# Values of four heads in one projection: 512 weight columns moving, half of the tokens at a time

## The chip, the cores and the metric

The kernel runs on one core of a Trainium2 chip. The metric is device time in microseconds of one launch; lower is better. Matrix products run on TensorE (PE in the profile), their results lie in eight PSUM banks of 128 x 512 floats; VectorE (DVE), ScalarE (ACT) and GpSimd (POOL) do elementwise work; SyncE (SP) issues nearly all DMAs, in one queue and in order.

## The reference

One decoder layer, all in float32, for 1024 tokens of width 2048, with 8 stick-breaking heads and 8 retention heads of 128 columns each:

```python
mod = silu(c) @ w_ada + b_ada                       # shift, scale, gate
h   = rms_norm(x, norm_gain) * (1 + scale) + shift  # 1024 x 2048
proj = h @ w_in                                     # 2048 x 8192
q_sb, k_sb, v_sb, z_sb, q_r, k_r, v_r, z_r = split(proj)   # 1024 columns each
oa = stick_breaking(rms_norm(q_sb), rms_norm(k_sb), v_sb) * silu(z_sb)
ob = group_norm(retention(rotary(q_r), rotary(k_r), v_r)) * silu(z_r)
out = x + gate * (concat(oa, ob) @ w_out)
```

## The kernel before

Every large product is made from two float32r parts of each operand, a high part and the exact rest, in three matmuls (`mm3`, L132): high by high, high by low, low by high. The normed and conditioned input is kept as `h_hi` and `h_lo`, transposed (2048 features on partitions, in 16 blocks `kc`), in SBUF for the whole projection. Weights are streamed: `wchunk` (L124) takes a raw tile of 128 x 512 floats (tag `wr`, three buffers), loads 256 KB into it from SP's queue, and `split_w` (L116) makes the high part on ACT (L119) and the low part on DVE (L121), each in one of three buffers (tags `wh` and `wl`). Weight chunks are given a high priority (`AHEAD`), so that the scheduler of ACT, DVE and SP places them early. TensorE's order is the order of the program.

Two kinds of unit use this stream. `unit_t` (L139) makes one head's 128 columns of queries, keys or z, transposed: weights stationary, 512 tokens moving, two PSUM banks (tag `pj`, four banks), four chunks of four feature blocks. `unit_v` (L156) makes values, tokens by columns: 128 tokens stationary, 256 weight columns (two heads) moving, two blocks of tokens to a bank, so that the eight blocks of tokens fill the four `pj` banks; eight chunks of two feature blocks. There are eight such units, `v0`, `v2`, `v4`, `v6` and `rv0`, `rv2`, `rv4`, `rv6`.

The units are TensorE's steady work. After every second block each of them yields, and `tick` (L181) then lets the waiting tasks take a step: the norms of queries and keys, the heads' attention, and in the retention stage `z_bias` (L506) and `gate_parts` (L529). A task says after how many ticks it wants to go on. `z_bias` is started just before the first retention values; it loads 32 pieces of `w_in` into raw tiles of the tag `wr` (L516), two a step, a step every second tick, and sums them on DVE (L519, L521). `gate_parts` is started just behind the first retention values; it loads 64 pieces of `w_ada` into the same raw tiles (L490), one every third tick, eight to a part, and sums them on DVE (L494, L496).

What becomes of the values differs by stage. For the stick-breaking heads `spill_v` (L571) copies the four banks to staging tiles (tag `T`, four buffers, shared with the attention's `a_hi` and `a_lo`) and writes them to DRAM (`vraw`), from where `load_v` (L599) brings each head's values back. For the retention heads `evac_v` (L457) copies the banks straight into the two heads' tiles (tag `V`, two buffers). The retention attention (L797) first turns keys (`turn_k`), and after a gap of five ticks uses the values in `states` (L812), then `scores`, `values` and `finish`. Each retention head's queries and keys are rotated (L787) with cosines and sines that are loaded once, at the start of the retention stage (L784, L785).

At the end `out_unit` (L749) makes the output, 512 columns of `w_out` moving and tokens stationary, with a raw tile for each chunk of weights; its first two parts, `0a` and `0b`, take half of the tokens each and also load the concatenated heads back from DRAM through raw tiles (L742).

Of the kernel before, what the change touches and what calls it, by code (L numbers as in the profile page):

```python
# [55 lines left out]
def layer_kernel(ctx, tc, x, c, w_ada, b_ada, norm_gain, w_in, sb_q_gain, sb_k_gain, ret_norm_gain, w_out,  # L56
# [50 lines left out]
    def rsqrt_newton(y, m, u, iters=3):  # L107
        """y = m ** -0.5 from the exponent trick and Newton's iteration (u is room for a product)."""
        nc.vector.tensor_scalar(y.bitcast(I32), m.bitcast(I32), -0.5, RSQRT_MAGIC, op0=ALU.mult, op1=ALU.add)
        for _ in range(iters):  # L110
            nc.vector.tensor_tensor(u, y, y, op=ALU.mult)
            nc.vector.scalar_tensor_tensor(u, u, -0.5, m, op0=ALU.mult, op1=ALU.mult)
            nc.vector.scalar_tensor_tensor(y, u, 1.5, y, op0=ALU.add, op1=ALU.mult)

# [22 lines left out]
    h_hi, h_lo = {}, {}  # by block of 128 features and half of the tokens  # L137

    def unit_t(col0, halves, name, lo_pool=()):  # L139
        """(w_in[:, col0:col0+128]).T @ h.T, 512 tokens a bank. Yields between its steps; returns the banks."""  # L140
        o = {hf: ps.tile([P, HALF], F32, tag="pj", bufs=4, name=f"pj_{name}_{hf}") for hf in halves}
        for kq in range(4):
            def parts(raw):
                yield raw.rearrange("p (k n) -> p k n", n=P), w_in_k[:, 4 * kq:4 * kq + 4, col0:col0 + P]
            with tc.high_priority(AHEAD):
                hi, lo = wchunk(parts, f"{name}_{kq}", nc.gpsimd if kq in lo_pool else nc.vector)
            for hf in halves:
                for k in range(4):
                    kc = 4 * kq + k
                    sl = slice(k * P, (k + 1) * P)  # L150
                    mm3(o[hf], hi[:, sl], lo[:, sl], h_hi[kc, hf], h_lo[kc, hf], kc == 0, kc == KC - 1)
                    if k % 2:
                        yield
        return o

    def unit_v(col0, name):  # L156
        """h @ w_in[:, col0:col0+256]: two heads' values, two blocks of tokens a bank."""
        o = [ps.tile([P, HALF], F32, tag="pj", bufs=4, name=f"pv_{name}_{b}") for b in range(4)]
        for kk in range(8):
            def parts(raw):  # L160
                yield raw.rearrange("p (k n) -> p k n", n=2 * P), w_in_k[:, 2 * kk:2 * kk + 2, col0:col0 + 2 * P]
            with tc.high_priority(AHEAD):
                hi, lo = wchunk(parts, f"{name}_{kk}")
            for tb in range(NB):
                for k in range(2):
                    kc = 2 * kk + k
                    sl = slice(k * 2 * P, (k + 1) * 2 * P)
                    tk = slice(tb % 4 * P, (tb % 4 + 1) * P)
                    mm3(o[tb // 2][:, (tb % 2) * 256:(tb % 2) * 256 + 256],
                        h_hi[kc, tb // 4][:, tk], h_lo[kc, tb // 4][:, tk], hi[:, sl], lo[:, sl],  # L170
                        kc == 0 and tb % 2 == 0, kc == KC - 1 and tb % 2 == 1)
                if tb % 2:
                    yield
        return o

    # The projections are TensorE's steady work; the heads' tasks put their small products between
    # its steps, each some steps after the one whose results it needs.
# [31 lines left out]
    # The conditioning's scale is loaded before its shift. Until the shift is known h.T stands without it,  # L209
    # and what is projected from that (the first NZ retention heads' z) gets its share later (z_bias).  # L210
# [5 lines left out]
    vraw = [dr.tile([P, NB, 2, P], F32, name=f"vraw{i}") for i in range(NH // 2)]  # L216
    zb = cons.tile([P, 8], F32, name="zb")
    with tc.tile_pool(name="st", bufs=1) as st:
# [7 lines left out]
        def load_ada(cc, gs=range(4)):  # L226
            """A chunk of 256 columns of w_ada: eight chunks of the scale, then eight of the shift."""
            col = (D if cc < 8 else 0) + (cc % 8) * 2 * P
            for g in gs:
                ada[cc, g] = ar = st.tile([P, 4, 2 * P], F32, tag="ada", bufs=ADA_BUFS, name=f"ada_{cc}_{g}")  # L230
                nc.sync.dma_start(ar, ada_rows[:, 4 * g:4 * g + 4, col:col + 2 * P])
# [12 lines left out]
        def x_scale(ts, ss):  # L244
            """x over its rows' root mean squares, for some blocks of tokens."""
# [15 lines left out]
        def x_turn(kc, g, tag, bufs):  # L261
            """Half of a block of x.T, into the place that the next block of h.T's low part takes over."""
# [10 lines left out]
        def ada_sums(cc):  # L273
            """Sums of silu(c) w_ada over a partition's sixteen rows, for a chunk of 256 columns."""
# [20 lines left out]
        def ada_mod(cc, acc):  # L295
            """Sums over the partitions: (scale + 1) gain, or shift, for two blocks of h.T."""
# [10 lines left out]
        def make_h(kc, hf):  # L307
            """h.T without its shift."""
# [149 lines left out]

    def evac_v(o, idx):
        vt = []  # L460
        for e in range(2):
            v = com.tile([P, NB, P], F32, tag="V", bufs=2, name=f"v_{idx + e}")
            vt.append(v)
        with tc.high_priority(AHEAD):
            for b in range(4):
                src = o[b].rearrange("p (t e n) -> p t e n", t=2, e=2)
                for e in range(2):
                    dst = vt[e][:, 2 * b:2 * b + 2, :]
                    nc.scalar.activation(dst, src[:, :, e, :], AF.Copy)  # L469
        return vt  # L470
# [13 lines left out]
    def gate_part(h, pool):  # L484
        """The gate's columns 256 h to 256 (h + 1), without their bias, to gate_row."""
# [22 lines left out]
    def z_bias():  # L508
        """The shift's share in the first NZ retention heads' z, to zb."""
# [56 lines left out]
    def split_r(r, name):  # L566
        """A tile's two exact parts, by halves."""
        parts = [com.tile([P, S], F32R, tag="R", bufs=6, name=f"{n}_{name}") for n in ("rh", "rl")]
        return parts

    def spill_v(o, h, pool):  # L571
        """Two heads' values to DRAM, as they stand in the banks."""
        with tc.high_priority(AHEAD):
            for b in range(4):
                vt = pool.tile([P, HALF], F32, tag="T", bufs=4, name=f"vt_{h}_{b}")
                nc.scalar.activation(vt, o[b], AF.Copy)
                nc.sync.dma_start(vraw[h // 2][:, 2 * b:2 * b + 2].rearrange("p t e n -> p (t e n)"), vt)
# [3 lines left out]
    def sb_attention(h, q, k, pool, gap):  # L581
        # The heads' steps: a block of 128 queries over a chunk of 512 keys. Two blocks of queries
        # go together into the product with the values.
# [15 lines left out]
        def load_v():  # L599
            assert done_heads[0] == h  # L600
            for hf in range(2):
                bl = slice(hf * 4, hf * 4 + 4)
                raw = wp.tile([P, 4, P], F32, tag="wr", bufs=3, name=f"vr_{h}_{hf}")
                nc.sync.dma_start(raw, vraw[h // 2][:, bl, h % 2, :])
                nc.scalar.activation(v_hi[:, bl], raw, AF.Copy)
                nc.vector.tensor_tensor(v_lo[:, bl], raw, v_hi[:, bl].bitcast(F32), op=ALU.subtract)
# [32 lines left out]
        def turn(s):  # L639
            """Transposes into banks of two blocks of keys by two blocks of queries; after the second, splits."""  # L640
# [61 lines left out]
    vs = {}  # L702
    with tc.tile_pool(name="sb", bufs=1) as sb:
        for h in range(NH):
# [15 lines left out]
            if h % 2 == 0:  # L720
                spill_v(steady(unit_v(2 * GW + h * P, f"v{h}")), h, sb)
            start(sb_attention(h, q, k, sb, SB_GAP if h < NH - 1 else 2))

        # The first retention head's queries and keys, under the last stick-breaking head.
# [24 lines left out]
    def out_unit(n, tbs, name, finish, half=None, tail=2):  # L749
        """y[:, 512 n:512 (n + 1)] for some blocks of tokens, a bank each (half: of concat, to be loaded too)."""  # L750
# [29 lines left out]
    with tc.tile_pool(name="rt", bufs=1) as rt:  # L780
# [16 lines left out]
        def ret_attention(h, q, k, v, z, gap):  # L797
# [76 lines left out]
            if z is None:  # L874
# [4 lines left out]
                for hf in range(2):  # L879
# [3 lines left out]
                    nc.vector.scalar_tensor_tensor(zh, zh, zb[:, h:h + 1], sw, op0=ALU.add, op1=ALU.mult)  # L883
            turn_k(0)
# [17 lines left out]
        for h in range(NH):  # L902
# [19 lines left out]
            if h % 2 == 0:  # L922
                vs[h], vs[h + 1] = evac_v(steady(unit_v(6 * GW + h * P, f"rv{h}")), NH + h)
            if h == 0:
                start(gate_parts(rt))
            if h < NH - 1:
                start(ret_attention(h, q, k, vs.pop(h), z, RT_GAP))

# [1 line left out]
        start(ret_attention(NH - 1, q, k, vs.pop(NH - 1), z, 2))  # L930
# [80 lines left out]
```

## Time and profile before

| what | value |
|---|---|
| median of 3 runs | 2157.64 us (2153.45 to 2159.12) |
| profiled execution, span of its instructions | 2156.7 us |
| what the runs' median has beyond that span | 0.9 us |
| TensorE busy, matmuls | 2066.9 us (96%), 11167 |
| VectorE, ScalarE, GpSimd busy | 56%, 35%, 16% |
| moved by DMA | 224.29 MB, mean 104 GB/s |

The page gives no time of the profiled execution from launch to end; its span stands for it. A group's line names the source line, the engine, the operation, what it writes and reads, its shape and count, then busy time and mean duration, then the engine's idle time before the group and what ended it. Matmuls overlap, so a mean duration of a matmul is a latency; the rate of a run of matmuls is the distance between their starts in the timeline. In an answer about one tile, a row gives least, median and greatest duration in ns and the first and last start in us. In the rows of a queue, SPq, the first number is the time of issue.

### The profile page before, as it was taken

The numbers are of one execution on the slowest core, as the hardware profiler recorded it, in microseconds if no ns is written. First come the engines' busy times: TensorE is split into PE (matmuls) and PEld (weight loads), VectorE is DVE, ScalarE is ACT, GpSimd is POOL, SyncE is SP. The second block draws the span as 40 slices with busy tenths as digits, with TensorE's granted clock in tenths as the row PEclk, the third lists the DMA queues.
The fourth block names the chain that finished last, engine by engine and source line by source line (L and its number), as shares of the span: only waits on it lengthen the run. The fifth ranks groups of instructions, "written<-read, shape, count | busy, mean of one in ns | idle before, by whom it ended". The sixth has DMA issues, their size and how long they took to land.

```text
span 2156.7 us, 29735 instructions
## 1 busy us (share of the span) xinstructions
PE 2066.9 (96%) x11167; PEld 1771.6 (82%) x11167; DVE 1212.4 (56%) x2270; ACT 744.9 (35%) x1424; POOL 340.0 (16%) x475
## 2 busy tenths in 40 slices
PE   4878899999999999999999999999999999999998
PEld 3656779888988898888988988988988988688887
DVE  6999774477448653865386556556355146523132
ACT  6655442444235433543254222223232123311110
POOL 3654330111011201120111101011011010000000
PEclk9989999999999999999999999999999999999999
DMA  8847511221222112121212533433232124734132
GB/s 281 297 153 231 181 49 59 79 69 45 64 69 74 50 59 74 56 62 59 74 50 77 168 117 96 132 97 115 89 96 62 54 62 146 223 104 132 49 127 78
DMA packets 232404, 224.29 MB, mean 104 GB/s; under 512 B 12674, under 2 KB 187844, under 8 KB 232260
## 3 DMA queue, kind: packets, MB, share of 16 engines
q1 hardware_dynamic: 231872, 222.36, 32.8%
q8 instruction: 87, 1.43, 0.3%
q14 instruction: 57, 0.47, 0.1%
q10 hardware_dynamic: 388, 0.04, 0.0%
HBM read 194.03 MB, written 28.32 MB: 103 GB/s over the span
## 4 chain that ended last, share of the span: by engine, by line
PE 73%; DVE 13%; DMA 5%; issue 4%; ACT 3%; POOL 1%; ACTq 0%; SPq 0%; DVEq 0%; POOLq 0%
PE y L134 4%; PE y L135 4%; PE y L133 4%; PE pv_v L135 3%; PE pv_v L134 3%; PE pv_v L133 3%; PE pj_rq L133 3%; PE pj_rq L135 3%; PE pj_rq L134 3%; PE pj_rk L133 3%; PE pj_rk L135 3%; PE pj_rk L134 3%; PE pj_q L134 2%; PE pj_z L133 2%; PE pj_q L133 2%
## 5 line engine op out<-in xcount | busy, mean ns | idle before, releaser
L133 PE MATMUL pv_rv<-wh_rv,h_hi 128*128 128x256 f32 x512 | 146.5, 286 | 3.5 <-ACT wh_rv L119 3.5
L133 PE MATMUL y<-wh_o,c_hi 128*128 128x512 f32 x384 | 149.4, 389 | 0.0
L134 PE MATMUL y<-wl_o,c_hi 128*128 128x512 f32 x384 | 149.4, 389 | 0.0
L135 PE MATMUL y<-wh_o,c_lo 128*128 128x512 f32 x384 | 149.4, 389 | 0.0
L134 PE MATMUL pv_rv<-wl_rv,h_hi 128*128 128x256 f32 x512 | 146.1, 285 | 0.8 <-DVE wl_rv L121 0.7
L134 PE MATMUL pv_v<-wl_v,h_hi 128*128 128x256 f32 x512 | 144.9, 283 | 0.0
L133 PE MATMUL pv_v<-wh_v,h_hi 128*128 128x256 f32 x512 | 144.9, 283 | 0.0
L135 PE MATMUL pv_rv<-wh_rv,h_lo 128*128 128x256 f32 x480 | 136.4, 284 | 0.0
L135 PE MATMUL pv_v<-wh_v,h_lo 128*128 128x256 f32 x480 | 135.8, 283 | 0.0
L121 DVE TENSOR_TENSOR wl_o<-wr_o,wh_o 128x512 fp32r<-128x512 f32 x48 | 33.2, 692 | 180.3 <-ACT wh_o L119 180.3
L632 DVE TENSOR_TENSOR_SCAN om<-om 128x128 f32<-128x128 f32 (+2 forms) x96 | 96.2, 1002 | 43.6 <-POOL om L622 42.3
L119 ACT ACTIVATE wh_o<-wr_o 128x512 fp32r<-128x512 f32 x48 | 30.3, 632 | 220.7 <-PE y L135 216.3
L133 PEld LDWEIGHTS pv_rv<-wh_rv,h_hi 128*128 128x128 f32 x512 | 98.8, 193 | 4.9 <-ACT wh_rv L119 3.9
L133 PE MATMUL pj_rq<-h_hi,wh_rq 128*128 128x512 f32 x256 | 102.6, 401 | 0.3 <-ACT v L469 0.3
L133 PE MATMUL pj_rk<-h_hi,wh_rk 128*128 128x512 f32 x256 | 102.3, 400 | 0.0
L283 POOL TENSOR_TENSOR acc_p<-acc_p,ada 128x256 f32<-128x256 f32 x96 | 87.0, 907 | 96.9 <-ACT ada L282 68.0
L133 PE MATMUL pj_z<-h_hi,wh_z 128*128 128x512 f32 x256 | 101.3, 396 | 0.0
L133 PE MATMUL pj_q<-h_hi,wh_q 128*128 128x512 f32 x256 | 100.7, 393 | 0.0
L135 PE MATMUL pj_q<-h_hi,wl_q 128*128 128x512 f32 x256 | 100.6, 393 | 0.0
L134 PEld LDWEIGHTS pv_rv<-wl_rv,h_hi 128*128 128x128 f32 x512 | 98.9, 193 | 1.8 <-DVE wl_rv L121 1.6
L133 PE MATMUL pj_k<-h_hi,wh_k 128*128 128x512 f32 x256 | 100.2, 392 | 0.0
L135 PE MATMUL pj_rq<-h_hi,wl_rq 128*128 128x512 f32 x256 | 100.1, 391 | 0.0
(273 smaller groups left out, 5820.9 us busy)
## 6 DMA issues: line engine op xcount, KB each, us to landing
ada<-in_w_ada_dram SPq DMA_DIRECT2D x64, 512.0 KB
gr<-in_w_ada_dram SPq DMA_DIRECT2D x64, 256.0 KB
wr_o<-in_w_out_dram SPq DMA_DIRECT2D x48, 256.0 KB
x<-in_x_dram SPq DMA_DIRECT2D x32, 256.0 KB
wr_rz<-in_w_in_dram SPq DMA_DIRECT2D x32, 256.0 KB
wr_q<-in_w_in_dram SPq DMA_DIRECT2D x32, 256.0 KB
wr_k<-in_w_in_dram SPq DMA_DIRECT2D x32, 256.0 KB
wr_z<-in_w_in_dram SPq DMA_DIRECT2D x32, 256.0 KB
```

What stands on the lines that cost most here:

```text
L119: nc.scalar.activation(hi[:, 0:n], raw, AF.Copy)
L121: lo_eng.tensor_tensor(lo[:, 0:n], raw, hi[:, 0:n].bitcast(F32), op=ALU.subtract)
L133: nc.tensor.matmul(o, a_hi, b_hi, start=first, stop=False)
L134: nc.tensor.matmul(o, a_hi, b_lo, start=False, stop=False)
L135: nc.tensor.matmul(o, a_lo, b_hi, start=False, stop=last)
L283: nc.gpsimd.tensor_tensor(acc_p, acc_p, src, op=ALU.add)
L632: nc.vector.tensor_tensor_scan(rev, rev, rev, init, op0=ALU.mult, op1=ALU.bypass)
```

## The change

`unit_v` now makes the values of four heads at a time for half of the tokens: 512 weight columns move, each of four blocks of tokens has a bank of its own, and a chunk holds one feature block. To cover all tokens it is called twice (`hf` 0 and 1), and streams the same weights both times. A new function, `project_v`, calls it, copies the four banks of each half to staging tiles and writes them to `vraw`, which now holds four heads to a piece; it replaces `spill_v` and `evac_v`. It is called at heads 0 and 4 of each stage. In the stick-breaking stage its staging tiles are those of tag `T` as before; in the retention stage they are a new pair (tag `vt`, two buffers). Each retention head loads its values from `vraw` into its tile when its attention starts. Yields remain after every second block: a pass over half of the tokens has 16 chunks with two yields each. Comments and docstrings are removed, which shifts line numbers.

```diff
-    vraw = [dr.tile([P, NB, 2, P], F32, name=f"vraw{i}") for i in range(NH // 2)]
+    vraw = [dr.tile([P, NB, 4, P], F32, name=f"vraw{i}") for i in range(NH // 2)]
...
-    def unit_v(col0, name):
-        o = [ps.tile([P, HALF], F32, tag="pj", bufs=4, name=f"pv_{name}_{b}") for b in range(4)]
-        for kk in range(8):
+    def unit_v(col0, hf, name):
+        o = [ps.tile([P, HALF], F32, tag="pj", bufs=4, name=f"pv_{name}_{hf}_{b}") for b in range(4)]
+        for kc in range(KC):
             def parts(raw):
-                yield raw.rearrange("p (k n) -> p k n", n=2 * P), w_in_k[:, 2 * kk:2 * kk + 2, col0:col0 + 2 * P]
+                yield raw, w_in_k[:, kc, col0:col0 + HALF]
             with tc.high_priority(AHEAD):
-                hi, lo = wchunk(parts, f"{name}_{kk}")
-            for tb in range(NB):
-                for k in range(2):
-                    kc = 2 * kk + k
-                    sl = slice(k * 2 * P, (k + 1) * 2 * P)
-                    tk = slice(tb % 4 * P, (tb % 4 + 1) * P)
-                    mm3(o[tb // 2][:, (tb % 2) * 256:(tb % 2) * 256 + 256],
-                        h_hi[kc, tb // 4][:, tk], h_lo[kc, tb // 4][:, tk], hi[:, sl], lo[:, sl],
-                        kc == 0 and tb % 2 == 0, kc == KC - 1 and tb % 2 == 1)
+                hi, lo = wchunk(parts, f"{name}_{hf}_{kc}")
+            for tb in range(4):
+                tk = slice(tb * P, (tb + 1) * P)
+                mm3(o[tb], h_hi[kc, hf][:, tk], h_lo[kc, hf][:, tk], hi, lo, kc == 0, kc == KC - 1)
                 if tb % 2:
                     yield
...
-    def evac_v(o, idx):
...
-    def spill_v(o, h, pool):
...
+    def project_v(col0, i, name, stage):
+        for hf in range(2):
+            o = steady(unit_v(col0, hf, name))
+            with tc.high_priority(AHEAD):
+                for b in range(4):
+                    vt = stage(f"vt_{name}_{hf}_{b}")
+                    nc.scalar.activation(vt, o[b], AF.Copy)
+                    nc.sync.dma_start(vraw[i][:, 4 * hf + b].rearrange("p e n -> p (e n)"), vt)
...
-                nc.sync.dma_start(raw, vraw[h // 2][:, bl, h % 2, :])
+                nc.sync.dma_start(raw, vraw[h // 4][:, bl, h % 4, :])
...
-            if h % 2 == 0:
-                spill_v(steady(unit_v(2 * GW + h * P, f"v{h}")), h, sb)
+            if h % 4 == 0:
+                project_v(2 * GW + h * P, h // 4, f"v{h}",
+                          lambda name: sb.tile([P, HALF], F32, tag="T", bufs=4, name=name))
...
+            v = com.tile([P, NB, P], F32, tag="V", bufs=2, name=f"v_{h}")
+            nc.sync.dma_start(v, vraw[2 + h // 4][:, :, h % 4, :])
             turn_k(0)
             yield gap
             states(0)
...
-            if h % 2 == 0:
-                vs[h], vs[h + 1] = evac_v(steady(unit_v(6 * GW + h * P, f"rv{h}")), NH + h)
+            if h % 4 == 0:
+                project_v(6 * GW + h * P, 2 + h // 4, f"rv{h}",
+                          lambda name: rt.tile([P, HALF], F32, tag="vt", bufs=2, name=name))
```

More of the change, by code (lines that the diff above doesn't have):

```diff
@@ L457, in r_tile @@
         return com.tile([P, S], F32, tag="R", bufs=6, name=name)
-    def evac_v(o, idx):
[L460 to L470, printed above, removed]
     def silu_evac(o, dst, halves):
@@ L569, in split_r @@
         return parts
-    def spill_v(o, h, pool):
[L573 to L577, printed above, removed]
+    def project_v(col0, i, name, stage):
[6 more added lines that the diff above has]
+                    nc.sync.dma_start(vraw[i][:, 4 * hf + b].rearrange("p e n -> p (e n)"), vt)
     done_heads = [0]
@@ L795, in rotate, with ret_attention @@
                 nc.vector.tensor_tensor(r[:, sl], r[:, sl], sw, op=ALU.add)
-        def ret_attention(h, q, k, v, z, gap):
+        def ret_attention(h, q, k, z, gap):
             f = NH + h
@@ L926, in layer_kernel @@
             if h < NH - 1:
[L927 to L930 removed]
+                start(ret_attention(h, q, k, z, RT_GAP))
+        start(ret_attention(NH - 1, q, k, z, 2))
         done = []
```

1 line of the change is left out of this document (removed).

## The prediction

> **What bounds the kernel now.** I read the page first (span, busy shares, costliest groups), then TensorE's timeline inside one value projection and inside the output projection, then each value unit by its tile, and last the queues around the slowest of these units.
>
> ```profile
> span 2156.7 us, 29735 instructions
> ...
> PE 2066.9 (96%) x11167; PEld 1771.6 (82%) x11167; DVE 1212.4 (56%) x2270; ACT 744.9 (35%) x1424; POOL 340.0 (16%) x475
> ...
> L133 PE MATMUL pv_rv<-wh_rv,h_hi 128*128 128x256 f32 x512 | 146.5, 286 | 3.5 <-ACT wh_rv L119 3.5
> L133 PE MATMUL y<-wh_o,c_hi 128*128 128x512 f32 x384 | 149.4, 389 | 0.0
> ...
> L133 PE MATMUL pv_v<-wh_v,h_hi 128*128 128x256 f32 x512 | 144.9, 283 | 0.0
> ```
>
> TensorE is busy for 96% of the span and everything else has room, so the kernel runs at the rate of TensorE's instruction stream, wherever the weights reach it in time. The means of 286 and 389 ns are latencies of overlapping matmuls; the rate is the distance from start to start, which only the timeline shows. First a value projection (256 columns moving), then the output projection (512 columns moving, and like the changed values with tokens as the stationary operand):
>
> ```profile
> 599.95 0.28 PE L135 MATMUL pv_v<-wh_v,h_lo 128*128 128x256 f32 x1
> ...
> 602.83 0.28 PE L135 MATMUL pv_v<-wh_v,h_lo 128*128 128x256 f32 x1
> ```
>
> ```profile
> 1999.76 0.39 PE L135 MATMUL y<-wh_o,c_lo 128*128 128x512 f32 x1
> ...
> 2003.84 0.39 PE L135 MATMUL y<-wh_o,c_lo 128*128 128x512 f32 x1
> ```
>
> Between the first two rows lie 24 starts: 2.88 / 24 = 0.120 us a matmul. Between the others lie 18: 4.08 / 18 = 0.2267 us. Twice 0.120 is 0.240, so a wide matmul saves 0.0133 us against two narrow ones.
>
> Three units by their first and last starts (value unit 1 of the stick-breaking heads, value unit 0 of the retention heads, second part of the first output column block):
>
> ```profile
> L133 PE MATMUL pv_v<-wh_v,h_hi x128: 278/283/283, 559.0 to 606.2; 128*128 128x256 f32 x128
> ...
> L133 PE MATMUL pv_rv<-wh_rv,h_hi x128: 278/283/415, 1194.5 to 1247.7; 128*128 128x256 f32 x128
> ...
> L133 PE MATMUL y_0b<-wh_o0b,c_hi x64: 388/389/505, 1837.4 to 1889.1; 128*128 128x512 f32 x64
> ```
>
> A value unit is 384 matmuls, 46.1 us at 0.120. The first took 47.5 us (606.2 plus three starts, less 559.0) with the products of an attention head in between, so it is dense. The second took 53.6 us with nothing in between: 7.5 us were lost to late weights. There `z_bias` takes the same three raw tiles (tag wr) for its 32 loads.
>
> **The change part by part.**
>
> *Matmuls.* Before, 8 units x 384 = 3072 narrow matmuls: 3072 x 0.120 = 368.6 us. After, four groups of four heads, each in two passes over half of the tokens, 16 chunks x 4 blocks x 3 = 192 matmuls a pass: 8 x 192 = 1536 wide ones, 1536 x 0.2267 = 348.2 us. **-20.4 us**, on the engine that sets the end. The price is that of the output projection, whose operands have the same shapes and come from SBUF in the same way; I see no row that would make it more than the 0.227 measured there.
>
> By the Trainium skill's page "TensorE: Matmul & The Clock Gate", section "Back-to-back issue gap", a warm matmul costs its columns at 2.4 GHz and about 2.5 ns. From that rule 256 columns are an estimated 109 ns and 512 an estimated 216 ns, the gain would be 4 us instead of 20, and the sum below would end some 16 us later. The trace differs: 120 and 227 ns.
>
> *The weights, twice.* A chunk stays 256 KB, but there are 128 instead of 64, and a chunk now feeds 12 matmuls, 2.72 us, instead of 48 x 0.120 = 5.76 us. Each chunk costs one ACT copy and one DVE subtraction (0.63 and 0.69 us in the rows below): 64 more are 40 us on ACT (35% busy) and 44 us on DVE (56%). Off the path, hidden by TensorE's stream, if three raw tiles turn over fast enough. In a pass that has them for itself they turn over once in three chunks, 8.2 us. One turn (issue, landing, copy, subtraction) takes:
>
> ```profile
> 1230.68 0.38 SPq L127 DMA_DIRECT2D wr_rv<-in_w_in_dram  x1
> 1232.30 3.84 SPq L516 DMA_DIRECT2D zw<-in_w_in_dram  x4
> 1236.85 0.38 SPq L127 DMA_DIRECT2D wr_rv<-in_w_in_dram  x1
> ```
>
> ```profile
> 1233.62 0.63 ACT L119 ACTIVATE wh_rv<-wr_rv 128x512 fp32r<-128x512 f32 x1 [5.51 <-DMA wr_rv<-in_w_in_dram]
> 1240.96 0.63 ACT L119 ACTIVATE wh_rv<-wr_rv 128x512 fp32r<-128x512 f32 x1 [6.71 <-DVE zb_acc L521]
> ```
>
> ```profile
> 1234.29 0.69 DVE L121 TENSOR_TENSOR wl_rv<-wr_rv,wh_rv 128x512 fp32r<-128x512 f32 x1 [1.08 <-ACT wh_rv L119]
> ...
> 1241.62 0.69 DVE L121 TENSOR_TENSOR wl_rv<-wr_rv,wh_rv 128x512 fp32r<-128x512 f32 x1 [0.69 <-ACT wh_rv L119]
> ```
>
> From 1230.68 to 1234.98 it is 4.30 us, from 1236.85 to 1242.31 it is 5.46 us. Both are under 8.2, so I cost six of the eight passes at nothing beyond their matmuls.
>
> *The first retention pass.* Here the same does not hold. `z_bias` steps every second tick, and a chunk now has two ticks instead of four, so per chunk it takes two raw tiles of the three. In the built order the SP queue then reads wr, zw, zw, wr, zw, zw, and each weight chunk waits for the subtraction of the chunk just before it: one tile is left for the weights, and a chunk costs a whole turn instead of 2.72 us. How many chunks this hits: the first three are in SBUF when the pass starts, the fourth is issued about then and split some 4.2 us later, so the fifth, a turn behind, is ready about 8.5 us into the pass, before its matmuls are due at 4 x 2.72 = 10.9. Behind it in DVE's order stands the rotation of the first head, which waits for the cosines:
>
> ```profile
> 1198.39 0.33 SPq L784 DMA_DIRECT2D cos<-in_rot_dram  x1
> ```
>
> ```profile
> 1204.84 0.69 DVE L794 TENSOR_TENSOR rq<-rq,cos 128x512 f32<-128x512 f32 x1 [2.64 <-DMA cos<-in_rot_dram]
> 1207.46 0.69 DVE L795 TENSOR_TENSOR rq<-rq,sw_q 128x512 f32<-128x512 f32 x1 [1.92 <-POOL sw_q L793]
> ```
>
> From the issue to the end of the first rotated half there passed 9.8 us, and subtractions queued on DVE stand behind it. In the new order the cosines are issued right behind the fifth chunk's load, about 4.6 us into the pass, so the first rotated half ends at 14.4 us, and the sixth chunk's copy and subtraction bring it to about 16. Ten more follow at a turn each. At 4.5 us (nearer the short end, since each weight load now comes ahead of the two bias loads, not behind four) the last is ready at 16 + 45 = 61 and used up at 63.7 us. Dense, the pass is 16 x 2.72 = 43.5. So 20.2 us are lost where 7.5 were: **+12.7 us**. Ends: 4.30 gives 61.7 us (+10.7), 5.46 gives 73.3 us (+22.3).
>
> *Between the halves.* The second pass needs all four banks again. In the stick-breaking stage four staging tiles take the copies as banks finish, 0.68 us apart, and a bank is needed 2.7 us after its last matmul: nothing. In the retention stage there are two staging tiles, so the third copy waits for the first one's write; and after the starved pass the next chunk is issued only when the last one has been split. I put 1.7 us for the first unit and 1.2 us for the second: **+3** (0 to 6). The write's time is from these rows, a value unit's last copy, its write, the load behind it, and that load's first user:
>
> ```profile
> 387.61 0.50 SPq L577 DMA_DIRECT2D vraw<-vt  x1
> 391.31 0.37 SPq L604 DMA_DIRECT2D vr<-vraw  x1
> ```
>
> ```profile
> 386.95 0.60 ACT L576 ACTIVATE vt<-pv_v 128x512 f32<-128x512 f32 x1 [0.84 <-PE pv_v L135]
> ...
> 394.83 0.63 ACT L605 ACTIVATE vh<-vr 128x512 fp32r<-128x512 f32 x1 [2.97 <-DMA vr<-vraw]
> ```
>
> *Retention values through DRAM.* `evac_v` copied into the heads' tiles; now a head's values come back as one 512 KB load, issued when its attention starts. For six heads they are in DRAM long before, and the load has five ticks (6.8 us at 6 matmuls a tick). For heads 0 and 4 the chain is new: last copy, write (3.7 us from issue to the load's issue, above), load (3.5 us for 256 KB, so 3.5 to 4.7). The last copy itself waits for a staging tile. Counted from the pass's end: copy at 2 to 3.3 us, write issued at 3 to 4, load issued at 5.5 to 7.7, values there at 9 to 12.4. `states` stands in TensorE's order 8.6 us after the pass (six ticks and four transposes). So TensorE, and behind it the next head's queries, wait 0.4 to 3.8 us: **+4** for the two (0 to 8). On SP the load holds back the next key weights, which are needed some 13 us later: nothing.
>
> *Gate loads.* In the second retention unit `gate_parts` takes raw tiles too: 8 loads in 28 ticks, so 0.57 a chunk of two ticks. A load keeps its tile for two DVE instructions of about 0.5 us and no ACT copy:
>
> ```profile
> 1249.00 1.53 DVE L496 SCALAR_TENSOR_TENSOR ga<-gr,silu_c,ga 128x256 f32<-128x256 f32 x3
> ```
>
> At 1.57 tiles a chunk a tile may take 2.72 / 1.57 = 1.73 us. The output part above had two tiles a chunk (weights and concat) and got 16 chunks in 51.7 + 0.7 = 52.4 us, 1.64 us a tile. Just enough: **+1** (0 to 13).
>
> *At nothing:* fewer, wider copies out of PSUM in the retention stage; 25 MB more traffic on a mean of 104 GB/s; the first attention starting a unit later (TensorE's ticks are the same in number, so its stream is only reordered).
>
> Sum: -20.4 + 12.7 + 3 + 4 + 1 = +0.3 us on a span of 2156.7. The median of the runs is 2157.64, 0.9 above that span, so I forecast **2158 us**. No change here means within 0.3%, 6.5 us, about what three runs that spread over 2153.45 to 2159.12 can tell.
>
> **The rivals.**
>
> *Faster: the first retention pass is not starved.* If loads, copies and subtractions of neighbouring chunks overlap so that a turn costs no more than 3.2 us, the pass ends at 51 us, loses as much as the unit before, and the sum is -12.4: **2145 us**. For it: the matmul gain rests on two plain rows, and each weight load now stands ahead of its bias loads. Against it: no turn shown is under 4.30 us, and the raw tile of each chunk is that of the chunk before. From 3.8 us down it is faster than 0.3%.
>
> *Slower: the gate loads starve the second retention unit.* Place: both its passes; the point is 1.73 us a tile, and the sum is slower by 0.3% from about 1.87. At 2.0 us a tile a chunk takes 3.14 us, 32 x 0.42 = 13.4 us instead of 1: **2170 us**. For it: the output part shows no better than 1.64, and there the writes of the staging tiles and the values' loads do not stand in the same queue. Against it: a gate load needs no ACT copy, so its turn is shorter than the two kinds in the output part.
>
> *Slower: the longest turn.* At 5.46 us in the first pass the sum is 9.6 us more, **2168 us**. TensorE's clock could add to it:
>
> ```profile
> 1210.00:1220.00 10.00, 6.87 (x43) 6.47 (x42) 7.99 (x10) 3.14 (x5) 5.01 (x4) 0.83 0.47 142
> ```
>
> One long gap in this stretch (PE busy 6.87 of 10 us) cost granted clock, 0.83. Gaps of 1.8 us a chunk are shorter, so I add nothing.
>
> *The gain is not there.* If a wide matmul cost all but as much as two narrow ones, 0.0133 us less would shrink to a few ns; with 4 us of gain left the time is **2174 us**. It would take a fixed part per matmul of 2 to 3 ns, where two rows show 13 ns. The skill's rule above is this case.
>
> **How the numbers follow.** Forecast (sum within 6.5 us of nothing) 0.44; first pass not starved 0.25; gate loads 0.20; longest turn 0.08; no gain 0.03. So faster 0.25, same 0.44, slower 0.31. The range reaches from the faster rival's 2145, less 1, to 2 above the gate rival's 2170: 2144 to 2172.
>
> **What would show it right or wrong.** Wide value matmuls 0.227 us apart. The first retention pass 62 to 66 us long, TensorE waiting there for wh_rv and wl_rv some 20 us in all, its second pass about 45. The other six passes 43.5 us plus the attention products between them. The state updates of heads 0 and 4 waiting 0.4 to 3.8 us for the values' load. If the first pass ends near 51 us, the turn was mis-sized; if passes of the second retention unit take over 46 us, the gate loads were; if the stick-breaking passes are not dense, the three raw tiles do not suffice even alone, and the whole reading of the turn is wrong.

## The result, and the profile after

| | before | after |
|---|---|---|
| median of the runs | 2157.33 us (2153.45 to 2159.12, 4 runs) | 2167.95 us (2162.81 to 2170.01, 4 runs) |
| profiled execution, span | 2156.7 us | 2160.9 us (its own time 2162.81) |
| matmuls | 11167 | 9631 |

After takes 1.0051 of the time before [1.0035, 1.0067]. Run again, it was 1.0038 [1.0025, 1.0051], 2164.84 us against 2155.5. One of those five repeats, 2322.32 us at a granted clock of 0.84, is a slow run and is not counted. So the change costs some 8 to 11 us: a little over the 0.3% that I called no change, and 7 to 10 us above the forecast of 2158. The two traces differ by 4.2 us only; the profiled run of after is the fastest of its four.

From the page of after, the span, the engines' shares, and the groups of the value matmuls by high part (busy time, mean ns, then TensorE's idle time before them):

```profile
span 2160.9 us, 27067 instructions
...
PE 2053.7 (95%) x9631; PEld 1689.3 (78%) x9631; DVE 1254.5 (58%) x2334; ACT 782.4 (36%) x1472; POOL 339.5 (16%) x475
...
L133 PE MATMUL pv_rv<-wh_rv,h_hi 128*128 128x512 f32 x256 | 103.1, 403 | 9.9 <-ACT wh_rv L119 7.8
...
L133 PE MATMUL pv_v<-wh_v,h_hi 128*128 128x512 f32 x256 | 99.7, 390 | 1.6 <-DVE zt L701 1.6
```

TensorE has 1536 matmuls fewer and 13.2 us less busy time, yet the span is longer. The idle time before the group of the retention values grew from 3.5 to 9.9 us in this one group of three, and the group's mean of 403 ns stands above the 390 of the stick-breaking stage with the same shapes. Next, TensorE's timeline inside a value pass of the stick-breaking stage:

```profile
399.67 0.39 PE L134 MATMUL pv_v<-wl_v,h_hi 128*128 128x512 f32 x1
...
401.70 0.39 PE L134 MATMUL pv_v<-wl_v,h_hi 128*128 128x512 f32 x1
```

Nine starts in 2.03 us, 0.2256 us each: the wide matmul costs what the output projection promised. So the loss is in what stands around the matmuls. The two retention units by their tile, pass by pass (least, median and greatest ns, first and last start), in three stretches: first unit's first pass (two rows; in the first of them the last start is already the first of the second pass), its second pass, and both passes of the second unit:

```profile
L133 PE MATMUL pv_rv<-wh_rv,h_hi x65: 387/389/628, 1186.1 to 1250.5; 128*128 128x512 f32 x65
...
L135 PE MATMUL pv_rv<-wh_rv,h_lo x60: 388/389/628, 1189.3 to 1249.4; 128*128 128x512 f32 x60
...
L133 PE MATMUL pv_rv<-wh_rv,h_hi x64: 389/389/494, 1250.5 to 1295.5; 128*128 128x512 f32 x64
...
L133 PE MATMUL pv_rv<-wh_rv,h_hi x128: 387/389/630, 1509.4 to 1605.8; 128*128 128x512 f32 x128
```

From the first start of the first pass to that of the second it is 64.4 us, where 192 matmuls at 0.2267 us are 43.5: 20.9 us are lost. The last 0.8 us of them lie behind the first pass's last matmul (1249.4). The second pass is over at 1296.2, three starts behind its last high-by-high product, after 45.7 us with 14 products of an attention in between. The second unit, 97.1 us to its end at 1606.5, splits at 1558.3 into 48.8 and 48.2 us. SP's queue in the first pass shows why, and so do ACT and DVE for one chunk:

```profile
1216.79 0.33 SPq L127 DMA_DIRECT2D wr_rv<-in_w_in_dram  x1
1217.45 0.86 SPq L498 DMA_DIRECT2D zw<-in_w_in_dram  x2
1220.87 0.33 SPq L127 DMA_DIRECT2D wr_rv<-in_w_in_dram  x1
1221.53 0.86 SPq L498 DMA_DIRECT2D zw<-in_w_in_dram  x2
1225.02 0.33 SPq L127 DMA_DIRECT2D wr_rv<-in_w_in_dram  x1
```

```profile
1219.49 0.63 ACT L119 ACTIVATE wh_rv<-wr_rv 128x512 fp32r<-128x512 f32 x1 [3.45 <-DMA wr_rv<-in_w_in_dram]
```

```profile
1220.15 0.69 DVE L121 TENSOR_TENSOR wl_rv<-wr_rv,wh_rv 128x512 fp32r<-128x512 f32 x1 [2.20 <-ACT wh_rv L119]
```

A weight chunk is issued every 4.08 and 4.15 us, and the next issue (1220.87) comes 0.03 us after the end of the subtraction of the chunk before (1220.15 + 0.69). Issue, landing, copy and subtraction stand one behind the other, with two bias loads between: one raw tile for the weights, where a chunk's matmuls last 2.72 us.

Two more losses. In the first, the attention of head 0 waits for the values' load; SP's queue first, then TensorE:

```profile
1299.51 0.34 SPq L561 DMA_DIRECT2D vraw<-vt_rv  x1
...
1303.60 0.61 SPq L869 DMA_DIRECT2D v<-vraw  x1
```

```profile
1304.62 0.39 PE L135 MATMUL pj_rq<-h_hi,wl_rq 128*128 128x512 f32 x1
1308.08 1.13 PE L800 MATMUL up<-v,kd 128*128 128x128 f32 x8 [3.06 <-DMA wr_rk<-in_w_in_dram]
```

The load is issued 7.4 us behind the pass's end, and 1.4 us later (1304.62 + 0.39) TensorE has nothing else to do and stands for 3.06 us. The releaser named there is a weight load that was issued behind the values' load; `states` does not read it, it reads `v`. The second is the handover of the banks in the second unit: TensorE, ACT, and a window of TensorE's clock (length, then busy time of PE, PEld, DVE, ACT and POOL, then PEclk, share of the DMA engines and GB/s):

```profile
1559.54 0.40 PE L135 MATMUL pv_rv<-wh_rv,h_lo0s 128*128 128x512 f32 x1
1561.47 0.50 PE L133 MATMUL pv_rv<-wh_rv,h_hi 128*128 128x512 f32 x1 [1.53 <-ACT vt_rv L560]
```

```profile
1560.82 0.60 ACT L560 ACTIVATE vt_rv<-pv_rv 128x512 f32<-128x512 f32 x1 [1.59 <-DMA vraw<-vt_rv]
```

```profile
1562.00:1566.00 4.00, 3.90 (x11) 2.68 (x10) 0.69 (x1) 1.11 (x2) 0.00 (x0) 0.59 0.53 195
```

The third bank's copy waits for a staging tile whose write is under way, TensorE waits for that copy, and behind the gap of 1.93 us the granted clock is 0.59 for 4 us: 11 matmuls start where at 0.2267 us there is room for 17.6.

### The profile page after: what moved, and what is told of

It reads as the page before. It is cut to its first block, busy times and chain, and to the rows that moved or that the text cites. A ratio compares the mean times of both kernels' runs of the same rounds, so it can differ in the third digit from the quotient of the medians.

```text
span 2160.9 us, 27067 instructions
## 1 busy us (share of the span) xinstructions
PE 2053.7 (95%) x9631; PEld 1689.3 (78%) x9631; DVE 1254.5 (58%) x2334; ACT 782.4 (36%) x1472; POOL 339.5 (16%) x475
## 4 chain that ended last, share of the span: by engine, by line
PE 69%; DVE 13%; DMA 9%; issue 4%; ACT 4%; POOL 1%; SPq 0%; ACTq 0%; DVEq 0%; POOLq 0%
PE y L135 4%; PE y L133 4%; PE y L134 4%; PE pv_v L133 3%; PE pv_v L135 3%; PE pv_v L134 3%; PE pj_rq L133 2%; PE pj_rq L135 2%; PE pj_rq L134 2%; PE pj_q L134 2%; PE pj_q L135 2%; PE pj_q L133 2%; PE pj_rk L133 2%; PE pj_rk L135 2%; PE pj_rk L134 2%
## 5 line engine op out<-in xcount | busy, mean ns | idle before, releaser
L133 PE MATMUL pv_rv<-wh_rv,h_hi 128*128 128x512 f32 x256 | 103.1, 403 | 9.9 <-ACT wh_rv L119 7.8
L134 PE MATMUL pv_rv<-wl_rv,h_hi 128*128 128x512 f32 x256 | 103.4, 404 | 5.4 <-DVE wl_rv L121 5.3
L121 DVE TENSOR_TENSOR wl_v<-wr_v,wh_v 128x512 fp32r<-128x512 f32 x64 | 44.3, 692 | 107.3 <-ACT wh_v L119 107.3
L133 PE MATMUL pv_v<-wh_v,h_hi 128*128 128x512 f32 x256 | 99.7, 390 | 1.6 <-DVE zt L701 1.6
L135 PE MATMUL pj_rk<-h_hi,wl_rk 128*128 128x512 f32 x256 | 100.0, 390 | 0.0
L135 PE MATMUL pj_k<-h_hi,wl_k 128*128 128x512 f32 x256 | 99.9, 390 | 0.0
L135 PE MATMUL pj_z<-h_hi,wl_z 128*128 128x512 f32 x256 | 99.8, 390 | 0.0
L134 PE MATMUL pv_v<-wl_v,h_hi 128*128 128x512 f32 x256 | 99.6, 389 | 0.0
```

The costliest lines, as they stand in the source:

```text
L121: lo_eng.tensor_tensor(lo[:, 0:n], raw, hi[:, 0:n].bitcast(F32), op=ALU.subtract)
L133: nc.tensor.matmul(o, a_hi, b_hi, start=first, stop=False)
L134: nc.tensor.matmul(o, a_hi, b_lo, start=False, stop=False)
L135: nc.tensor.matmul(o, a_lo, b_hi, start=False, stop=last)
```

## The experiments

Ratios are to before, with their 95% interval, from runs on the same chip as those of before beside them. The repeat of after ran on the chip of the three kernels below it in the table; the others ran on two other chips, without after beside them, so what they gain on after is read from the ratios.

| kernel | median us | ratio |
|---|---|---|
| after, again | 2164.84 | 1.0038 [1.0025, 1.0051] |
| change in the stick-breaking stage alone | 2150.70 | 0.9973 [0.9962, 0.9984] |
| change in the retention stage alone | 2170.49 | 1.0068 [1.0055, 1.0080] |
| after, bias loads in other tiles | 2150.93 | 0.9975 [0.9964, 0.9986] |
| after, bias loads half as often | 2158.18 | 1.0001 [0.9989, 1.0012] |
| after, more staging tiles | 2157.61 | 1.0007 [0.9998, 1.0016] |
| after, values of heads 0 and 4 used later | 2162.67 | 1.0035 [1.0021, 1.0048] |
| after, no gate loads in the second unit | 2162.73 | 1.0034 [1.0022, 1.0046] |
| after, four of these edits | 2145.22 | 0.9947 [0.9934, 0.9960] |
| after, bias loads and staging | 2140.20 | 0.9923 [0.9909, 0.9936] |

**After once more.** To see whether the passages above are there in another execution.

> The changed kernel once more, for a tighter interval and a second trace. The stage account of the first trace gives +4 us on the span; the runs' median gave +10.6. Theory (the account by stages holds, runs differ by short stretches of half clock and by queueing): ratio 1.003 to 1.006, first retention pass again 63 to 66 us with some 20 us lost. Rival (something the first trace did not show, of 6 us more): a passage that is longer here by more than 3 us than in the first trace.

By the tile of the retention values, the first pass:

```profile
L133 PE MATMUL pv_rv<-wh_rv,h_hi x65: 387/393/760, 1186.6 to 1250.8; 128*128 128x512 f32 x65
```

64.2 us again. The other three took 46.7, 49.8 and 48.4 us (45.7, 48.8 and 48.2 in the first trace). The losses belong to the kernel. The rival's condition is just met as well: from the first value projection to the first retention values it is 850.7 us here, 3.2 us more than in the first trace. Here the granted clock is 0.50 from 663.1 to 666.5 and from 1100.0 to 1103.4, where the first trace has no such stretch.

**Each stage alone.** The change made from before, for heads 0 to 7 of one kind only. In the stick-breaking kernel, from before:

```diff
-            if h % 2 == 0:
-                spill_v(steady(unit_v(2 * GW + h * P, f"v{h}")), h, sb)
+            if h % 4 == 0:
+                project_v(2 * GW + h * P, h // 4, f"v{h}",
+                          lambda name: sb.tile([P, HALF], F32, tag="T", bufs=4, name=name))
```

The other kernel is after, with the old `unit_v` and `spill_v` for these heads:

```diff
-            if h % 4 == 0:
-                project_v(2 * GW + h * P, h // 4, f"v{h}",
-                          lambda name: sb.tile([P, HALF], F32, tag="T", bufs=4, name=name))
+            if h % 2 == 0:
+                spill_v(steady(unit_n(2 * GW + h * P, f"v{h}")), h, sb)
```

> Wide values in the stick-breaking stage alone; the retention stage as before. Theory: 1536 narrow matmuls become 768 wide ones, 184.3 - 174.1 = -10.2 us, less 2 us for the wait of the first pass on z's banks: 2149 us, ratio 0.996. Rival (streaming the weights twice costs about what the wide matmul saves wherever it is done): within 0.2% of before.

> Wide values in the retention stage alone; the stick-breaking stage as before. Theory: -10.2 us of matmuls, +13 us in the first pass beside z_bias, +4 us for the values' loads of heads 0 and 4, +6 us in the second unit (gate loads, bank handover, half clock): 2170 us, ratio 1.006. Rival (the two stages share the loss): not slower than before by more than 0.3%.

The stick-breaking stage gains 5.8 us, the retention stage loses 14.7; together they lose 8.9, and the whole change lost 8.2 when it was run beside them. The two parts add up. The stick-breaking stage gains 2 us less than the 8 that I expected, still inside its interval [3.4, 8.2]. In that stage three of four passes are dense, 43.5 us. The first is not; in the trace of after, TensorE's timeline:

```profile
340.38 0.39 PE L135 MATMUL pv_v<-wh_v,h_lo0s 128*128 128x512 f32 x1
342.41 0.50 PE L133 MATMUL pv_v<-wh_v,h_hi 128*128 128x512 f32 x1 [1.63 <-DVE zt L701]
```

A block of tokens now opens its bank 0.68 us after the one before. The fourth is reached 2 us into the pass, and `z`'s silu on DVE has not left it yet. Before, two blocks shared a bank and a chunk held two feature blocks, so the fourth bank was opened after 36 matmuls, 4.3 us, and nobody waited. The gap costs 1.8 us.

**The bias loads in other tiles.** The theory of the one raw tile says that the first pass must be nearly dense if `z_bias` takes its pieces into wide tiles of another tag (`R`), as many loads and sums as before:

```diff
         for kc in range(KC):
+            both = r_tile(f"zw_{kc}")
             for i in range(2):
                 n = HALF if i == 0 else NZ * P - HALF
-                raw = wp.tile([P, HALF], F32, tag="wr", bufs=3, name=f"zw_{kc}_{i}")
+                raw = both[:, i * HALF:(i + 1) * HALF]
```

> The change, but the 32 loads of z_bias land in spare tiles of the tag R (a pair of loads to a tile of 128 x 1024) and no longer in the weights' raw tiles. Theory (one raw tile left for the weights makes a chunk cost a whole turn): the first retention pass takes 45 to 48 us instead of 64, the kernel 2149 to 2154 us, 16 us under the changed one, ratio to before 0.997. Rival (not the tiles, but the order on SP and DVE behind the bias loads and the rotation): the pass stays over 58 us.

The first pass by its tile, with what ended the idle time of TensorE and its weight loads, and SP's queue in it:

```profile
L133 PE MATMUL pv_rv<-wh_rv,h_hi x65: 388/389/496, 1191.7 to 1239.3; 128*128 128x512 f32 x65
...
  DVE wl_rv L121: 6.9, 8
```

```profile
1224.19 0.33 SPq L127 DMA_DIRECT2D wr_rv<-in_w_in_dram  x1
1224.57 1.62 SPq L499 DMA_DIRECT2D zw<-in_w_in_dram  x3
1227.17 0.33 SPq L127 DMA_DIRECT2D wr_rv<-in_w_in_dram  x1
```

47.6 us instead of 64.4, and 14 us off the time. The traffic is the same and denser in time, so neither the DMA engines nor the sums on DVE were short: the tiles were. What still is lost is 4.1 us, most of it in three waits of TensorE for subtractions on DVE (the 6.9 us of the row count its weight loads' waits too).

**The bias loads half as often.** The same theory from the other side: a step every fourth tick leaves two raw tiles to each weight chunk, and spreads `z_bias` over both passes.

```diff
-ZB_GAP = 2
+ZB_GAP = 4
```

> The change with one number changed: z_bias steps every fourth tick instead of every second, so its 32 loads spread over both passes of the first retention unit and a chunk shares the three raw tiles with one bias load, not two. Theory (a raw tile turns over in 4.2 to 4.3 us, so two tiles a chunk need 2 x 4.25 / 3 = 2.83 us where TensorE takes 2.72): first pass 48 to 52 us, second 45 to 48, kernel 8 to 13 us under the changed one. Rival (any bias load in the queue costs the same, only its passes move): the two passes together stay over 106 us.

The two passes took 53.5 and 48.0 us, 101.5 together against 110.1 in after; by the ratios the time fell by 8 to 11 us. Better, as the theory has it, but short of what I expected of the first pass. Two spacings of 3.4 and 3.3 us between starts remain, one inside it and one at its end, and behind the first a stretch of half clock, in TensorE's timeline and in windows as above:

```profile
1205.41 0.39 PE L135 MATMUL pv_rv<-wh_rv,h_lo 128*128 128x512 f32 x1
1208.86 0.79 PE L133 MATMUL pv_rv<-wh_rv,h_hi 128*128 128x512 f32 x1 [3.06 <-ACT wh_rv L119]
```

```profile
1208.90:1214.50 5.60, 5.60 (x13) 4.10 (x14) 5.45 (x7) 2.45 (x4) 2.43 (x2) 0.50 0.34 94
```

**More staging tiles.** Is the load of the values late because of itself, or because of the two staging tiles in front of it? Here the copies go to halves of wide tiles of tag `R`:

```diff
+        pair = []
+        def stage_r(name):
+            if not pair:
+                t = r_tile(name)
+                pair.extend([t[:, HALF:], t[:, 0:HALF]])
+            return pair.pop()
...
-                          lambda name: rt.tile([P, HALF], F32, tag="vt", bufs=2, name=name))
+                          stage_r)
```

> The change, but in the retention stage the four banks of a pass are copied to halves of two spare tiles of the tag R instead of the two staging tiles vt, so that the third copy waits for no write. Theory: the gap of 2 us at the start of the second pass of both retention units goes, and with it the half clock behind it in the second unit: that pass 44.5 instead of 48.3 us, in all -5 us against the changed kernel. Rival (the gap is ACT's order, copies standing behind the next weights): the gap of 2 us stays.

ACT, SP's queue and TensorE behind the first unit, whose last pass ended at 1298.1:

```profile
1296.30 2.64 ACT L560 ACTIVATE vt_rv<-pv_rv 128x512 f32<-128x512 f32 x4
```

```profile
1301.59 0.61 SPq L877 DMA_DIRECT2D v<-vraw  x1
```

```profile
1306.93 1.13 PE L808 MATMUL up<-v,kd 128*128 128x128 f32 x8
```

Four copies in a row. The load is issued 3.5 us behind the pass instead of 7.4, and TensorE no longer waits. The wait at the handover in the second unit is gone too: its second pass takes 44.3 us (48.2). The first unit's second pass is as it was, 45.7 us: what it waits for are weights, not staging tiles. In all some 7 us are saved, where I expected 5. One gap of 2.15 us with half clock behind it moved into the second unit's first pass, 50.2 us.

**Values of heads 0 and 4 used later.** Three more ticks before `states(0)` of these heads:

```diff
-            yield gap
+            yield gap + (3 if h % 4 == 0 else 0)
             states(0)
```

> The change, but heads 0 and 4 of the retention stage use their values three ticks later (eight instead of five ticks after the keys are turned). Theory: the waits of 3.1 and 0.9 us for the values' load go, nothing else changes: -4 us, the first query unit behind rv0 27 instead of 30 us. Rival (the wait is on the state's chain on DVE, not on the load): it moves along and stays.

The waits for the values are gone, the queries' projection behind the first unit takes 25.2 us where it took 30.0 (with 14 fewer attention products in it, which moved to the unit behind). I expected 4 us; by the ratios (1.0035 against 1.0038 and 1.0051) the time fell by 1 to 3 us, not more than the intervals.

**No gate loads in the second unit.** A flag set around the projection of the values lets `gate_part` load nothing there:

```diff
         for jj in range(8):
+            while in_v[0]:
+                yield 1
             gr = wp.tile([P, 2, n], F32, tag="wr", bufs=3, name=f"gr_{h}_{jj}")
```

> The change, but gate_parts loads nothing while the retention values of heads 4 to 7 are projected (it steps on afterwards). Theory: the first pass of that unit loses its 2.5 to 3.5 us and takes 46 to 46.5 us with the 22 products of the attention inside; the second keeps its gap of 2 us and the half clock: -3 us. Rival of the forecast (gate loads starve both passes): -8 us or more.

Both passes of the second unit by their tile:

```profile
L133 PE MATMUL pv_rv<-wh_rv,h_hi x128: 389/389/497, 1512.2 to 1601.2; 128*128 128x512 f32 x128
```

89.0 us from first to last start instead of 96.4: 3.0 us of it in the first pass (45.8 against 48.8), the rest in the second, where the handover lost its gap as well (43.9 against 48.2). I had not expected that: with the same two staging tiles the wait for their writes vanished with the gate loads. But the loads that were held back come afterwards: the values' loads of heads 0 and 4 now stop TensorE for 2.6 and 2.1 us (3.1 and 0.6 in after), each with a stretch of half clock behind it, and from the last value matmul of the second unit to the first of the output it is 187.1 us, where after takes 181.3. So 5.8 of the 7.4 us come back there, and the first pass of the first unit took 66.8 us in this trace. By the ratios (1.0034 against the repeat's 1.0038) the kernel gains about 1 us, which is inside the intervals.

**A version of these edits.** First all four (bias loads, staging, later use, no gate loads), then bias loads and staging alone:

> All four together: bias loads in spare R tiles, values staged in R tiles, gate loads paused in the second unit, values of heads 0 and 4 used three ticks later. Theory: of the matmuls' 20 us all but 4 to 5 us come out: 2138 to 2144 us, ratio to before 0.993. Rival (R tiles now short, the waits come back as waits for R): not under 2148 us.

> The change with the bias loads and the staging of the retention values in R tiles, gate loads and the use of the values as in the change. Theory: between the changed kernel less 14 and less 7 (their single gains add up to 21, of which 2 to 4 are the same half clock or were met twice): 2142 to 2147 us, ratio to before 0.994 to 0.996; pausing the gate loads and using the values later then add no more than 2 us, so this equals the version with all four within 3 us. Rival: the pause of the gate loads carries the rest, and this is 4 us or more over the version with all four.

Both beat before. All four edits gain 0.53% [0.40, 0.66], a little less than I forecast. The simpler kernel gains 0.77% [0.64, 0.91], a little more than I forecast, and 1.1 to 1.3% on after. From the simpler one's page:

```profile
span 2137.5 us, 27047 instructions
...
PE 2045.8 (96%) x9631; PEld 1687.8 (79%) x9631; DVE 1253.2 (59%) x2334; ACT 781.6 (37%) x1472; POOL 340.2 (16%) x475
```

Its four passes take 48.8, 45.2, 49.1 and 44.5 us, and the queries behind both units do not wait. The other two edits add nothing: with all four the passes take 46.6, 45.1, 45.8 and 43.5 us, 6.6 us less, but from the second unit to the output it is 186.4 us instead of 180.3, the price of the gate loads that were paused. The spans are 2138.5 and 2137.5. The medians lie 5 us apart in favour of the simpler one, where I expected at most 3; the two intervals overlap by a hair and the chips differ, so that it is better is not shown.

## Why the prediction was right, and where it was off

The change gave and took in the places that the prediction named; the sum, +0.3 us, came out some 8 to 11 us too low. The time is 0.51% and, repeated, 0.38% longer, against the 0.3% of my band for no change. So it lies inside the range, but in the part called slower, to which I gave 0.31, and none of my slower rivals put it there: three small terms were too small.

*Matmuls, -20.4 us: right.* 0.2256 us from start to start in the new values. By the rule that I set against it (the Trainium skill, "TensorE: Matmul & The Clock Gate", section "Back-to-back issue gap", which gives it there for a single isolated matmul) both widths would pay only about 2.5 ns beyond their columns, and half of the change, in the stick-breaking stage, would gain 2 us and lose the 1.8 of `z`'s bank. That stage alone gained 5.8 us [3.4, 8.2]; the trace and the run disagree with the rule, and the rival of the missing gain falls with it.

*First retention pass, +12.7: right, in size and in mechanism.* The pass ends 63.6 us after its start (1249.42 and one spacing of 0.23, less 1186.07), where 63.7 was forecast: 20.1 us lost, so +12.6. The steps hold too, by DVE's subtractions for the sixth, the seventh and the last two chunks:

```profile
1200.62 1.72 DVE L121 TENSOR_TENSOR wl_rv<-wr_rv,wh_rv 128x512 fp32r<-128x512 f32 x1
...
1207.83 0.68 DVE L121 TENSOR_TENSOR wl_rv<-wr_rv,wh_rv 128x512 fp32r<-128x512 f32 x1
...
1241.12 0.69 DVE L121 TENSOR_TENSOR wl_rv<-wr_rv,wh_rv 128x512 fp32r<-128x512 f32 x1 [2.38 <-ACT wh_rv L119]
1246.28 0.69 DVE L121 TENSOR_TENSOR wl_rv<-wr_rv,wh_rv 128x512 fp32r<-128x512 f32 x1 [3.27 <-ACT wh_rv L119]
```

The sixth chunk was split 16.3 us into the pass (16 forecast), and the ten behind it took 44.6 us, 4.46 each (4.5 forecast). That this mean is so close is luck: eight of the ten followed each other every 4.16 us, under the lower end of 4.30, and two longer steps made up for them, 6.2 us for the seventh chunk, behind the rotation of the keys, and 5.2 for the last. The clock also fell in this pass, which I had ruled out; a window of the trace of after, columns as above:

```profile
1208.00:1212.00 4.00, 3.43 (x8) 2.76 (x9) 3.93 (x5) 1.83 (x3) 1.78 (x1) 0.50 0.41 131
```

That cost nothing as far as the rows show, since at 1220.17 TensorE stood waiting for a weight chunk again. The kernel with the bias loads elsewhere shows the cause, -14 us. The faster rival needed a turn of 3.2 us and is out; so is the longest turn of 5.46 for every chunk.

*Stick-breaking passes at nothing: off by 1.8 us.* I asked whether the banks come free between the two halves, and did not ask it at the start of the first half, where `z`'s banks are taken over. Narrower spacing of the banks' first use turned a cover of 4.3 us into one of 2.

*Between the halves, +3: too small.* The first unit lost 0.8 us ahead of its second pass and 0.5 behind that pass's first matmul, waiting for weights, against the 1.7 that I gave it. The second lost 1.7 us in the gap, as the range allowed, and 2.0 us more to the clock behind it (ten spacings in 4.2 us from 1562.04, where 2.3 would do); I gave it 1.2. The prediction said of the clock that short gaps add nothing. That step failed: the rule was drawn from one window with a long gap, and no row showed that a gap of 2 us is safe. Together 5.0 us. In the second unit more staging tiles took the gap away, and so did pausing the gate loads; it took both, two staging tiles and gate loads in the queue, to make it.

*Values' loads, +4: right.* 3.2 and 0.8 us. The load left 7.4 us behind the pass (5.5 to 7.7 forecast), and its user followed 4.5 us later (3.5 to 4.7). That the staging tiles hold it back, as the working said, is shown by the kernel with more of them.

*Gate loads, +1: too small.* Stopping them shortens the second unit's first pass by 3.0 us, so the term is about 3. That the kernel would be faster by it is not shown, since the paused loads cost about as much later. The rival in which they starve the unit (13.4 us) did not come.

With these terms the sum is -20.4 + 1.8 + 12.6 + 5.0 + 4.0 + 3 = +6.0 us. Measured were +8.2 [5.4, 11.0] on the repeat and +11.0 [7.6, 14.5] at first; the traces from which the terms are read differ by 4.2. So the terms explain the repeat within its interval, and leave a few us of the first comparison open. Stretches of half clock that one run has and another has not, such as those at 663 and 1100 us in the repeat, may be part of it; no run settles that. What also was off is the offset: after's span and its own time are 1.9 us apart. I had put 0.9 between span and median, which suggests that before's profiled run took about 2158.6 and was not a run at its median.

## What to carry to other kernels

A moving operand of twice the width saves a fixed part against two narrow products (here 13 ns), but each streamed weight chunk then covers half the time: count the buffers that the stream really has at that rhythm. A second user that takes two of three buffers per chunk leaves one, and then every chunk costs load, copy and split in a row, whatever the engines' shares say. Before values take the way through DRAM, count the staging tiles against the banks that must come free in a row: two for four held back the next pass and the reload alike, and the cure cost nothing that the runs could show.

## What was not expected of the hardware

Half clock after a short gap. In after, a gap of 1.93 us was followed by 4 us at a granted clock of 0.59 (rows above), with matmuls 0.43 us apart. The Trainium skill's page "TensorE: Matmul & The Clock Gate", section "Why this matters for your kernels", asks to avoid idle gaps above about 3 us; this gap is shorter, 1.53 us idle, and the clock fell all the same. Nor does a gap of that length always bring it. In the kernel with bias loads half as often, the same handover had a gap of 2.39 us, longer, and the clock stayed whole:

```profile
1551.38 0.40 PE L135 MATMUL pv_rv<-wh_rv,h_lo0s 128*128 128x512 f32 x1
1553.77 0.51 PE L133 MATMUL pv_rv<-wh_rv,h_hi 128*128 128x512 f32 x1 [1.99 <-ACT vt_rv L560]
```

So the length of a gap alone does not decide. The traces show more of it. In each of them the granted clock changes only at marks that are a multiple of 3.413 us apart, in after at 1207.77, 1214.60, 1562.76 and 1566.17. Here are the step before and the step behind such a mark in after, and the two steps that share the longer gap in the other kernel:

```profile
1559.34:1562.76 3.42, 1.78 (x7) 0.87 (x6) 0.61 (x1) 1.19 (x2) 0.00 (x0) 1.00 0.95 316
1562.76:1566.17 3.41, 3.41 (x9) 2.63 (x9) 0.69 (x1) 0.63 (x1) 0.00 (x0) 0.50 0.40 152
```

```profile
1549.38:1552.79 3.41, 2.15 (x9) 1.11 (x7) 1.38 (x2) 1.69 (x4) 0.00 (x0) 1.00 0.68 217
1552.79:1556.21 3.42, 2.44 (x10) 1.76 (x11) 0.00 (x0) 1.73 (x3) 0.00 (x0) 1.00 0.94 326
```

In after the whole gap fell into one step, which left TensorE idle for 1.64 us of it (3.42 less 1.78), and the next step ran at half clock. In the other kernel a mark cut the gap in two, 1.26 and 0.98 us idle, and the clock stayed. Over all twelve traces, between 330 and 2100 us, each of the 14 full-clock steps with 1.87 us idle or more was followed by one at half clock, of the 20 with 1.63 to 1.87 us 13 were, and of those with less none. So what counts is how much of a gap falls between two marks. The marks do not stand still against the kernel: in the first retention pass the clock fell at 1207.77 in after and at 1202.40 in its repeat, no whole step apart. So a gap of 2 us should be priced between its own length and about 2 us more. What decides between 1.63 and 1.87 us stays open.
